# Attention scores on one core: the second rotary product of two key tiles in the two halves of TensorE's array

## The chip, the core and the metric

The kernel runs on one core of a Trainium2 chip. The core has five engines with a queue each: TensorE (PE) multiplies matrices on an array of 128 by 128 cells and writes its sums into PSUM, VectorE (DVE), ScalarE (ACT) and GpSimd (POOL) work element by element, and SyncE (SP) mostly issues DMA. A matmul consists of two instructions: a weight load (shown as PEld), which puts up to 128 x 128 values into the array, and the product itself, which streams up to 512 columns past them. The metric is the device time of one execution in microseconds; the median of three runs of the kernel before is 1282.82 us.

## What is computed

One layer of an encoder over 2048 tokens: an input projection, four heads of gated linear attention, four heads of latent attention with a rotary part, an output projection, a residual sum and a layer norm. The change concerns the scores of the latent attention:

```python
s = (jnp.einsum('bqhd,bkhd->bhqk', qn, k_nope, preferred_element_type=jnp.float32)
     + jnp.einsum('bqhr,bkr->bhqk', qr, k_r, preferred_element_type=jnp.float32))
p = jax.nn.softmax(s, axis=-1)
return jnp.einsum('bhqk,bkhv->bqhv', p.astype(v.dtype), v)
```

The rotary key `k_r` has 64 entries per token and is shared by the four heads; `qr` is the rotary query of one head.

## The kernel before

Float32 products are made from two parts. `hi` (L397) rounds a value to TensorE's fast 32-bit type on ACT, `lo` (L404) takes the rest as a second value of that type on DVE or POOL, and a product is the sum of high x high, high x low and low x high; low x low is left out (`mm3`, L452 to L456).

The program runs in stages. The sweeps over 128-token chunks project the input, do the linear attention and leave what the latent attention needs: in SBUF, for each of the 16 chunks (key tiles) `c`, the compressed keys `ckvT_h[:, c]` and `ckvT_l[:, c]` (128 x 128 each), their untransposed forms `vh`, `vl`, and one tile `kr[:, c]` (printed as krs) for the rotary key; in DRAM the absorbed queries and the rotary queries, high and low.

The rotary key has 64 entries, half of the array's rows. So `kr` stacks both parts: `c_krsh` (L1416, on ACT) writes the high part of a chunk's rotary key into columns 0 to 63 of a small tile, `c_krsl` (L1420, on POOL) the low part into columns 64 to 127, `c_tm` (L1433) transposes it on PE, and `c_krT` puts it into `kr[:, c]`: rows 0 to 63 hold the high part, rows 64 to 127 the low part. `fetch` (L1629) loads a query block's rotary part twice, into rows 0 to 63 and rows 64 to 127 of `rh` (high) and of `rl` (low). One product of `kr` with `rh` over all 128 rows thus gives (high + low) x high, and one with `rl` gives (high + low) x low.

Attention goes over 16 blocks (512 queries of one head), each over 8 pairs `j` of key tiles. `scores(i, j)` writes the two tiles of a pair into the two banks of one PSUM tile `pS` (two such tiles in rotation), five products of 512 columns each: three over the compressed part, `rh`, `rl`. Then `copy` brings both banks to SBUF in one ACT instruction (L1649), `smax` keeps the running maximum on DVE (L1662); once a block's 8 pairs are there the maximum is transposed and spread (`mx`, `mb`), subtracted on DVE (L1686), exponentiated on ACT (L1690), split on ACT (`phi`) and POOL (`plo`), and multiplied with the values on PE (`pv`, six products per pair into `o`). `acc` sums the exponentials on DVE and POOL. Blocks overlap: while one block's scores are made, the block before is in its softmax.

The order of all this is written by hand: the table `PLACE` gives each step a place in units of pairs, the steps are sorted by it, and `in_order` keeps every engine's instructions in that order. So no scheduler decides anything when a step becomes longer or shorter. The last block has its own table, and POOL also gets pieces of the output projection's preparation (`PLACE_OUT`) between the attention steps from block 9 on.

Of the kernel before, what the change touches and what calls it, by code (L numbers as in the profile page):

```python
# [92 lines left out]
    half=11.7,  # L93
# [296 lines left out]
class K:  # L390
# [1024 lines left out]

    def c_krsh(self, d):  # L1416
        d["krs"] = self.w1.tile([P, 2, 64], F32R, tag="krs", name=f"krs{d['c']}")
        self.hi(d["krs"][:, 0], d["kr"][:, 0])

    def c_krsl(self, d):  # L1420
        self.lo(d["krs"][:, 1], d["kr"][:, 0], d["krs"][:, 0], "pool")

    def c_vh(self, d):
        self.hi(self.vh[:, d["c"]], d["ckv"])
# [181 lines left out]
    def attention(self):  # L1606
        tc, nc = self.tc, self.nc
        mm = nc.tensor.matmul
        V, G, Ac = nc.vector, nc.gpsimd, nc.scalar
        NP = NKT // 2  # L1610
        with ExitStack() as ctx:
# [20 lines left out]
            def scores(i, j):  # L1632


                d = stt[i]
                qh, ql, rh, rl = d["q"]
                ps = d["ps", j] = pS.tile([P, 2, QB], F32, tag="pS", name=f"pS{i}_{j}")
                for e in range(2):
                    kh, kl, kr = (t[:, 2 * j + e] for t in (self.ckvT_h, self.ckvT_l, self.kr))
                    mm(ps[:, e], kh, qh, start=True, stop=False)  # L1640
                    mm(ps[:, e], kh, ql, start=False, stop=False)  # L1641
                    mm(ps[:, e], kl, qh, start=False, stop=False)  # L1642
                    mm(ps[:, e], kr, rh, start=False, stop=False)  # L1643
                    mm(ps[:, e], kr, rl, start=False, stop=True)  # L1644

            def copy(i, j):
                d = stt[i]
# [193 lines left out]
            for i in range(nb):  # L1841
                for j in range(NP):
                    t = NP * i + j
                    put(t, scores, i, j)
                    for n, f in (("copy", copy), ("max", smax), ("sub", sub), ("exp", exp), ("hi", phi), ("lo", plo),
                                 ("pv", pv), ("acc", acc)):
                        if n != "acc" or j != SUM_POOL[0] or i == nb - 1:
                            put(t + at(n, i, j), f, i, j)
                put(NP * i + at("acc0", i), acc0, i)
                for n, f in (("tmax", tmax), ("rmax", rmax), ("bmax", bmax)) + {nb - 1: (), nb - 2: own_late}.get(i, own):  # L1850
                    put(NP * i + NP - 1 + at(n, i), f, i)
                if i + 2 < nb:
                    put(NP * i + 4.05, fetch, i + 2)
# [103 lines left out]
            half = 5.44  # L1957
# [466 lines left out]
```

## Time and profile before

| what | value |
| --- | --- |
| median of 3 runs | 1282.82 us (1281.37 to 1285.22) |
| the profiled execution | 1283.54 us |
| its span, first to last instruction | 1281.7 us |
| mean granted TensorE clock | 0.998 |
| first and last score product | 607.9 and 1084.4 us |
| score products | 5 lines x 256 |
| copies of a pair (L1649) | 128 |

A row of a group reads: line, engine, operation, output<-inputs, shapes, count | busy time, mean ns of one | idle time of the engine just before, and who ended it. A row of the timeline begins with start and duration in us. Ends of matmuls are modelled: a matmul's duration overlaps its successor's, so what one costs is read from the starts. A row by stretches gives, for each engine, the busy time within the stretch and the number of instructions.

### The profile page before, as it was taken

What the parts mean: (1) busy time and instruction counts of PE and PEld (TensorE: products, weight loads), DVE (VectorE), ACT (ScalarE), POOL (GpSimd) and SP (SyncE); (2) the same over time, 40 slices, a digit from 0 to 9 for tenths busy, and PEclk for the clock granted to TensorE, in tenths of its full rate; (3) what the DMA queues carried; (4) which work ended last, traced back from release to release, by engine and by line L of the source; (5) the groups of instructions that cost most, each with busy time, mean ns of one, the idle gap of its engine ahead of it and who ended that gap; (6) DMA issues with size and microseconds to landing.
All of it is one profiled execution on the core that took longest, in us unless ns stands there. A gap on an engine that the chain in (4) does not pass through costs nothing.

```text
span 1281.7 us, 20184 instructions
## 1 busy us (share of the span) xinstructions
PE 1255.0 (98%) x6928; PEld 1108.3 (86%) x6928; DVE 941.1 (73%) x1702; ACT 876.2 (68%) x1553; POOL 852.7 (67%) x550
## 2 busy tenths in 40 slices
PE   7999999999999999999999999999999999999996
PEld 7999999999889999999788888888888888788875
DVE  7865775656675445555798888888888889648887
ACT  7765657666675665665588888888888888623355
POOL 0245555363657666672188888889999999955784
PEclk9999999999999999999999999999999999999999
DMA  8332525253675565555501111122213221468962
GB/s 299 98 92 63 177 71 172 87 155 101 195 244 159 180 225 189 181 194 166 175 1 41 42 42 41 42 58 58 59 58 91 53 52 33 173 211 304 343 196 84
DMA packets 122518, 166.81 MB, mean 130 GB/s; under 512 B 18502, under 2 KB 71118, under 8 KB 121776
## 3 DMA queue, kind: packets, MB, share of 16 engines
q1 hardware_dynamic: 114256, 163.39, 40.2%
q0 software_dynamic: 768, 2.10, 0.5%
q8 instruction: 55, 0.90, 0.4%
q10 hardware_dynamic: 7392, 0.03, 0.3%
q14 instruction: 47, 0.39, 0.2%
HBM read 106.72 MB, written 58.75 MB: 129 GB/s over the span
## 4 chain that ended last, share of the span: by engine, by line
PE 75%; DVE 6%; ACT 5%; POOL 4%; DMA 3%; issue 3%; SPq 0%; DVEq 0%; POOLq 0%; ACTq 0%
PE pS L1640 4%; PE pS L1641 4%; PE pS L1642 4%; PE pS L1643 4%; PE pS L1644 4%; PE o L454 4%; PE o L455 4%; PE o L456 4%; PE ipa L454 3%; PE ipa L456 3%; PE ipa L455 3%; PE pz L455 2%; PE pz L456 2%; PE pz L454 2%; PE ipg L454 2%
## 5 line engine op out<-in xcount | busy, mean ns | idle before, releaser
L406 POOL TENSOR_TENSOR pl<-s,ph 128x1024 fp32r<-128x1024 f32 x128 | 306.3, 2417 | 56.3 <-ACT ph L400 56.3
L1662 DVE TENSOR_TENSOR rm<-pS,rm 128x512 f32<-128x512 f32 x210 | 144.8, 690 | 26.4 <-ACT s L1649 20.8
L1686 DVE TENSOR_TENSOR s<-s,mb 128x1024 f32<-128x1024 f32 x128 | 151.3, 1214 | 9.4 <-PE mb L1680 9.3
L1649 ACT ACTIVATE s<-pS 128x1024 f32<-128x1024 f32 x128 | 131.3, 1026 | 37.7 <-PE pS L1644 33.4
L400 ACT ACTIVATE ph<-s 128x1024 fp32r<-128x1024 f32 x128 | 134.9, 1057 | 13.5 <-PE o L456 12.7
L1690 ACT ACTIVATE s<-s 128x1024 f32<-128x1024 f32 x128 | 131.5, 1050 | 13.4 <-DVE s L1686 13.3
L454 PE MATMUL ipa<-wah,xah 128*128 128x384 f32 (+1 forms) x384 | 129.8, 338 | 6.3 <-ACT wah L400 6.3
L1103 POOL TENSOR_TENSOR Us<-Us,cw 128x512 f32<-128x512 f32 x16 | 18.6, 1164 | 173.4 <-DVE Us L1101 157.9
L456 PE MATMUL ipa<-wah,xal 128*128 128x384 f32 (+1 forms) x384 | 124.8, 325 | 0.0
L455 PE MATMUL ipa<-wal,xah 128*128 128x384 f32 (+1 forms) x384 | 124.5, 324 | 0.1
L1640 PE MATMUL pS<-qh,ckvT_h 128*128 128x512 f32 x256 | 102.6, 401 | 0.8 <-DVE rm L1662 0.4
L454 PE MATMUL o<-ph,vh 128*128 128x512 f32 x256 | 101.1, 395 | 0.0
L1641 PE MATMUL pS<-ql,ckvT_h 128*128 128x512 f32 x256 | 99.9, 390 | 0.0
L1642 PE MATMUL pS<-qh,ckvT_l 128*128 128x512 f32 x256 | 99.9, 390 | 0.0
L1643 PE MATMUL pS<-rh,krs 128*128 128x512 f32 x256 | 99.8, 390 | 0.0
L1644 PE MATMUL pS<-rl,krs 128*128 128x512 f32 x256 | 99.8, 390 | 0.0
L456 PE MATMUL o<-ph,vl 128*128 128x512 f32 x256 | 99.8, 390 | 0.0
L455 PE MATMUL o<-pl,vh 128*128 128x512 f32 x256 | 99.7, 390 | 0.0
L1713 DVE TENSOR_TENSOR ap<-ap,s 128x512 f32<-128x512 f32 x120 | 83.1, 693 | 3.5 <-ACT s L1690 0.9
L454 PEld LDWEIGHTS ipa<-wah,xah 128*128 128x128 f32 x384 | 73.0, 190 | 7.1 <-ACT wah L400 6.5
L454 PE MATMUL pz<-xch,wzh 128*128 128x256 f32 x256 | 74.8, 292 | 0.0
L455 PEld LDWEIGHTS ipa<-wal,xah 128*128 128x128 f32 x384 | 73.0, 190 | 1.2 <-DVE wal L406 0.6
(446 smaller groups left out, 3902.2 us busy)
## 6 DMA issues: line engine op xcount, KB each, us to landing
xcf<-xT_dram SPq DMA_DIRECT2D x16, 512.0 KB, 4.7
xr<-x_dram SPq DMA_DIRECT2D x16, 512.0 KB, 6.3
xaf<-xT_dram SPq DMA_DIRECT2D x14, 512.0 KB, 3.8
wb<-wO_dram SPq DMA_DIRECT2D x16, 256.0 KB, 3.0
oib<-oi_s SPq DMA_DIRECT2D x16, 256.0 KB, 3.7
qdb<-qd_s SPq DMA_DIRECT2D x16, 256.0 KB, 4.8
SU<-su_s SPq DMA_DIRECT2D x16, 256.0 KB, 4.6
ub<-u_s SPq DMA_DIRECT2D x16, 256.0 KB, 4.2
```

The costliest lines, as they stand in the source:

```text
L400: return nc.scalar.activation(dst, src, AF.Copy).ins
L406: return e.tensor_tensor(dst, src, hi.bitcast(F32), ALU.subtract).ins
L454: mm(out, ah, bh, start=start, stop=False)
L455: mm(out, ah, bl, start=False, stop=False)
L456: mm(out, al, bh, start=False, stop=stop)
L1640: mm(ps[:, e], kh, qh, start=True, stop=False)
L1641: mm(ps[:, e], kh, ql, start=False, stop=False)
L1642: mm(ps[:, e], kl, qh, start=False, stop=False)
L1643: mm(ps[:, e], kr, rh, start=False, stop=False)
L1644: mm(ps[:, e], kr, rl, start=False, stop=True)
L1662: V.tensor_tensor(d["rm"], src[:, e], d["rm"], ALU.max)
L1686: V.tensor_tensor(s, s, d["mb"][:, None, :].to_broadcast([P, 2, QB]), ALU.subtract)
```

## The change

The product over `rl` is taken out of the loop over the two tiles of a pair and put behind it, and each of the two now uses 64 rows: the even tile rows 0 to 63, the odd tile rows 64 to 127 of `kr` and `rl`. So that these rows hold the high part in both cases, odd chunks get their high part in columns 64 to 127 and their low part in columns 0 to 63. The term low x low, which the products over 128 rows added, is no longer computed.

```diff
     def c_krsh(self, d):
         d["krs"] = self.w1.tile([P, 2, 64], F32R, tag="krs", name=f"krs{d['c']}")
-        self.hi(d["krs"][:, 0], d["kr"][:, 0])
+        self.hi(d["krs"][:, d["c"] % 2], d["kr"][:, 0])
 
     def c_krsl(self, d):
-        self.lo(d["krs"][:, 1], d["kr"][:, 0], d["krs"][:, 0], "pool")
+        p = d["c"] % 2
+        self.lo(d["krs"][:, 1 - p], d["kr"][:, 0], d["krs"][:, p], "pool")
...
                     mm(ps[:, e], kh, ql, start=False, stop=False)
                     mm(ps[:, e], kl, qh, start=False, stop=False)
                     mm(ps[:, e], kr, rh, start=False, stop=False)
-                    mm(ps[:, e], kr, rl, start=False, stop=True)
+                for e in range(2):
+                    half = slice(64 * e, 64 * e + 64)
+                    mm(ps[:, e], self.kr[half, 2 * j + e], rl[half], start=False, stop=True)
```

How PE's order changes is seen in the sixth block, where its sixth pair of scores is followed by the product of the block before with the values. Line numbers behind the edit are larger by one (sweep) or by three (from the second half of `scores` on). Before (pS is the pair's PSUM tile, o the output of the block before, the sizes are those of the result):

```order
L456 MATMUL o_9352<-ph_0_9278,vl 128x512
L1640 MATMUL pS_5_9368<-qh_8784,ckvT_h 128x512
L1641 MATMUL pS_5_9368<-ql_8786,ckvT_h 128x512
L1642 MATMUL pS_5_9368<-qh_8784,ckvT_l 128x512
L1643 MATMUL pS_5_9368<-rh_8788,krs 128x512
L1644 MATMUL pS_5_9368<-rl_8791,krs 128x512
```

The five rows of pS stand there twice, once per tile, and then `o` goes on. With the change, from the second tile's last compressed product on:

```order
L1643 MATMUL pS_5_9368<-qh_8784,ckvT_l 128x512
L1644 MATMUL pS_5_9368<-rh_8788,krs 128x512
L1647 MATMUL pS_5_9368<-rl_8791,krs 128x512 x2
L454 MATMUL o_9352<-ph_1_9313,vh 128x512
L455 MATMUL o_9352<-pl_1_9349,vh 128x512
L456 MATMUL o_9352<-ph_1_9313,vl 128x512
```

The first tile's product over rl has moved past four products of the second tile and stands next to the second tile's.

The other neighbour that the halves have is the transpose of a block's maximum, `mx`, in the first pair of the 15th block (`mx` and `o` belong to blocks before it). Before:

```order
L1643 MATMUL pS_0_11717<-rh_11304,krs 128x512
L1644 MATMUL pS_0_11717<-rl_11307,krs 128x512
L1668 MATMUL mx_11734<-ident,rm_11481 128x128 x4
L454 MATMUL o_11598<-ph_4_11642,vh 128x512
L455 MATMUL o_11598<-pl_4_11715,vh 128x512
```

With the change:

```order
L1644 MATMUL pS_0_11717<-rh_11304,krs 128x512
L1647 MATMUL pS_0_11717<-rl_11307,krs 128x512 x2
L1671 MATMUL mx_11734<-ident,rm_11481 128x128 x4
L454 MATMUL o_11598<-ph_4_11642,vh 128x512
L455 MATMUL o_11598<-pl_4_11715,vh 128x512
```

Nothing else moved here; the two products over rl stand between a product over all rows and a transpose. The instructions of ACT, DVE, POOL and SP stand in the same order with the same waits as before.

## The prediction

> **What bounds the kernel now.** I read the page first: busy times, then the chain of work that ended last.
>
> ```profile
> PE 1255.0 (98%) x6928; PEld 1108.3 (86%) x6928; DVE 941.1 (73%) x1702; ACT 876.2 (68%) x1553; POOL 852.7 (67%) x550
> PE 75%; DVE 6%; ACT 5%; POOL 4%; DMA 3%; issue 3%; SPq 0%; DVEq 0%; POOLq 0%; ACTq 0%
> L1640 PE MATMUL pS<-qh,ckvT_h 128*128 128x512 f32 x256 | 102.6, 401 | 0.8 <-DVE rm L1662 0.4
> L1643 PE MATMUL pS<-rh,krs 128*128 128x512 f32 x256 | 99.8, 390 | 0.0
> L1644 PE MATMUL pS<-rl,krs 128*128 128x512 f32 x256 | 99.8, 390 | 0.0
> L1649 ACT ACTIVATE s<-pS 128x1024 f32<-128x1024 f32 x128 | 131.3, 1026 | 37.7 <-PE pS L1644 33.4
> ```
>
> TensorE (PE) holds three quarters of the chain. The score products run 256 times per line: 16 blocks of 16 key tiles, 128 pairs (the copy at L1649, one per pair, says x128). In all of them PE sat idle 0.8 us before L1640 and 0.0 before the others, while ScalarE (ACT) waited 33.4 us for L1644. So within the attention stage the others wait for PE and PE for nobody. The busy times by stretch, from the first score to the last and then to the end, say the same and show who is next:
>
> ```profile
> core 0: us, PE busy (x) PEld busy (x) DVE busy (x) ACT busy (x) POOL busy (x), PEclk, DMA share, GB/s
> 607.90:700.00 92.10, 90.20 (x407) 73.27 (x406) 76.83 (x102) 69.55 (x78) 56.08 (x24) 1.00 0.26 78
> 700.00:800.00 100.00, 100.00 (x457) 82.58 (x457) 89.92 (x126) 84.61 (x95) 84.86 (x36) 1.00 0.16 40
> 800.00:900.00 100.00, 100.00 (x457) 82.67 (x456) 88.94 (x123) 84.41 (x95) 88.20 (x38) 1.00 0.19 51
> 900.00:1000.00 100.00, 100.00 (x460) 82.63 (x460) 88.01 (x122) 85.58 (x98) 92.88 (x41) 1.00 0.28 79
> 1000.00:1084.50 84.50, 84.50 (x385) 69.81 (x384) 76.89 (x107) 73.80 (x85) 83.25 (x40) 1.00 0.14 33
> 1084.50:1281.70 197.20, 186.41 (x837) 153.11 (x835) 145.23 (x226) 93.05 (x213) 135.01 (x89) 0.98 0.65 215
> ```
>
> PE is full in four of the five score stretches, at full granted clock (1.00). A nanosecond more per pair on PE is therefore a nanosecond of kernel; a nanosecond less counts only until GpSimd (POOL), busy 83.25 of 84.50 us in the last stretch, becomes the bound.
>
> What a matmul costs is not the 390 ns of the groups, since matmuls overlap. The timeline of one pair gives the step between starts (PEld are the weight loads):
>
> ```profile
> 709.15 0.39 PE L1640 MATMUL pS<-qh,ckvT_h 128*128 128x512 f32 x1
> ...
> 709.83 0.39 PE L1643 MATMUL pS<-rh,krs 128*128 128x512 f32 x1
> 709.84 0.19 PEld L1644 LDWEIGHTS pS<-rl,krs 128*128 128x128 f32 x1
> 710.06 0.39 PE L1644 MATMUL pS<-rl,krs 128*128 128x512 f32 x1
> ...
> 711.19 0.39 PE L1644 MATMUL pS<-rl,krs 128*128 128x512 f32 x1
> ...
> 711.87 0.39 PE L1642 MATMUL pS<-qh,ckvT_l 128*128 128x512 f32 x1
> ```
>
> From 709.15 to 711.87 lie twelve steps: 2.72 / 12 = 0.227 us each. A matmul prints 0.39 us, so 0.390 - 0.227 = 0.163 us of it runs under its successor. A weight load prints 0.19 us (187/188 ns at L1644) and runs under the matmul before it.
>
> **The change part by part.** *Removed and added.* Each pair loses two whole-array products over rl (2 x 0.227 us) and gains two products of half the rows, one in rows 0 to 63, one in rows 64 to 127. If the halves run side by side, both take one step of 0.227 us, since each still streams 512 columns. The gain is 0.227 us per pair, 128 x 0.227 = 29.0 us. If they run one after the other the gain is nothing.
>
> *The layout changes.* PE now goes from the whole array to halves and back, once per pair: 256 changes. No instruction of before uses half the rows, so I bound the price of one change by the nearest rows. The nearest odd shape is a four-column weight load, in the stretch behind the scores; a row of plain transposes stands beside it:
>
> ```profile
> 1106.75 0.39 PE L456 MATMUL o<-ph,vl 128*128 128x512 f32 x1
> 1106.98 0.27 PE L1785 MATMUL rt<-ident,rc 128*4 128x128 f32 x1
> 1107.01 0.48 PE L454 MATMUL o<-ph,vh 128*128 128x512 f32 x1
> 1107.32 0.40 PE L455 MATMUL o<-pl,vh 128*128 128x512 f32 x1
> ...
> 305.57 0.38 PE L984 MATMUL qT<-ident,q 128*128 128x128 f32 x2
> 305.79 0.38 PE L1019 MATMUL kT<-ident,k 128*128 128x128 f32 x2
> ```
>
> From 1106.75 to 1107.32 are 0.57 us; two steps of 0.227 leave 0.116 us for the odd shape, and a plain transpose takes (305.79 - 305.57) / 2 = 0.11 us. So that shape cost nothing extra: the low end is 0. (Below nothing it cannot go: a change computes nothing, and the shared step is counted above.) The high end: the array must first be empty, 0.163 us of tail exposed, and only then are the next weights loaded, 0.188 us: 0.351 us. I take 0.163 us: the odd shape keeps all 128 rows and writes one output at a time, so it asks for no such change as the halves do, and the tail is the one row that tells how long a product is still under way behind its step. That the loads are then hidden I take from the row at 709.84, where one runs fully under another matmul.
>
> *The second half's weights.* Two transposes 0.11 us apart show how closely weight loads can follow each other. The second half starts between 0 and 0.11 us behind the first; I take 0, as both loads (0.22 us) fit under the step of the matmul ahead. At the other end it is 14.1 us over 128 pairs.
>
> The Trainium skill bears on this in two places that speak against the change. Its page TensorEngine Tiling (Array Packing), section Key Properties, states that a change of tiling mode, unlike a change of tile, drains TensorE; no run here shows it yet. Its page TensorE: Matmul & The Clock Gate, section Single matmul latency, gives a lone warm matmul as (398 + N) / 2.4 ns, so 166 ns beyond the streaming, against the trace's 163 ns; by the page the sum below would be 128 x (2 x 0.166 - 0.227) = +13.4 us, an estimate.
>
> *What moves.* The first tile's bank closes four products later, 4 x 0.227 = 0.9 us. This costs nothing: its reader is the one copy over both banks (128x1024, L1649), which needs the second bank as well, and the maxima on VectorE (DVE) come behind the copy. Were the banks copied apart, the first copy would slide 0.9 us and with it the maximum. The other engines' orders and waits are the same as before. In the first pair, the two DMAs that bring rl are now waited for by one half each, later than before; nothing is late.
>
> *High and low swapped in odd tiles.* The same two instructions per chunk write the other 64 columns: same engines, shapes and count, cost 0; the transposes that follow read all 128 columns either way, and the product over rh sums both parts in either order.
>
> *Sum.* 128 x (2 x 0.163 - 0.227) = 41.7 - 29.0 = +12.7 us. The profiled execution took 1283.5 us for a span of 1281.7, 0.7 us above the median. 1283.5 + 12.7 - 0.7 = 1295.5 us. PE has no slack in these stretches to take it up (1.9 us idle in the first), and behind the last score the work follows PE in order.
>
> **The rivals.**
>
> *Faster: the change of layout is free and the halves run side by side.* Then PE loses 29.0 us over a stage of 476.6 us, 6.1%. The stretches would shrink from 92.1 to 86.5 and from 100 to 93.9 us in three, the third of these to 94.5 with POOL at 92.88; the last stretch stops at POOL's 83.25 (PE alone: 79.4). Together 5.6 + 6.1 + 6.1 + 5.5 + 1.2 = 24.5 us, so 1258.3 us; without POOL's limit 1253.8. For it speaks the odd shape that passed at 0.116 us; against it that no half of the rows was in use there. The rival holds while a change costs under 0.113 us (half of 0.227); at 0.05 us each, 1266.6 us. The Trainium skill, TensorE: Matmul & The Clock Gate, Part 3, has row tiles starting about 4 ns apart and four products of 32 rows done 3.07 times as fast; the halves would by that cost 0.231 us, an estimate of -28.5 us before POOL; it does not price the way back to the whole array.
>
> *Much slower: the weights are loaded behind the emptied array.* A change then costs 0.163 + 0.11 = 0.273 us (the closest loads seen) to 0.351 us: 256 x 0.273 - 29.0 = +40.9 and 256 x 0.351 - 29.0 = +60.9 us, 1323.7 to 1343.7 us. Halves that run one after the other between two drains of 0.163 us land there too, 256 x 0.163 = +41.7 us. For it: the loads now hide only because a matmul runs beside them. Against it: weights of another layout need not wait for sums of the old one to leave.
>
> *No change: the halves are treated as whole products.* One after the other, each 0.227 us, without price for a change: 1282.8 us. A change price near 0.113 us gives the same time. For it speaks that fewer rows have bought nothing so far: a product that reads 98 of them takes about as long as a transpose over 128.
>
> ```profile
> L925 PE MATMUL z<-lrTs,wg 98*128 98x128 f32 x64 | 9.1, 264 | 0.8 <-ACT lrTs L400 0.8
> L1668 PE MATMUL mx<-ident,rm 128*128 128x128 f32 x60 | 9.0, 272 | 0.3 <-DVE rm L1662 0.3
> ```
>
> Against it: 98 rows leave no room for a second product, 64 do; and for a price that just cancels the gain the window is narrow.
>
> **How the numbers follow.** Forecast (drain hidden loads, price 0.13 to 0.20 us, own range 1287 to 1305 us): 0.37. Much slower: 0.19. Faster: 0.36. No change: 0.08. A measurement of this kernel tells about 0.3% (3.9 us) from no change, 30 ns per pair. Faster by over 0.3%: 0.36; within: 0.08; slower: 0.37 + 0.19 = 0.56. The range takes in the faster rival's free end with POOL's limit, 1256, and the near end of the much slower one, 1325; what is left out is the rest of that one (some 0.12) and little below (0.03).
>
> **What would show it.** In the changed trace the two products over rl start within 0.01 us of each other if the halves run side by side, 0.11 us if the loads space them, 0.227 us if not at all. The starts from L1643's last product (L1644 there) to the first whole one behind the halves should be 2 x 0.227 + 2 x 0.163 = 0.78 us for the forecast, 0.45 us for the faster rival, 1.0 us or more for the much slower. PE should still be full in the score stretches and DVE, ACT and POOL show more idle time; if instead POOL fills the last stretch and PE waits at L455 for pl, the faster rival holds. The weight loads behind the halves show whether they start under them. The forecast is wrong if a change costs under 0.113 us or if the loads are exposed too.

## The result and the profile after

The changed kernel took 1304.4 us (median of 4 runs, 1303.9 to 1304.86) against 1283.0 us before: the ratio is 1.0165, with a 95% interval of 1.0148 to 1.0183. It is 21.4 us slower; 12.7 us were forecast. The profiled execution has a span of 1303.0 us, 21.3 us more than before.

Where the time went is seen in three stretches: up to the first score product, the score stage, and the rest. First the kernel before, then the changed one (columns as in the windows of the prediction):

```profile
0.00:607.60 607.60, 593.62 (x3933) 563.96 (x3934) 375.13 (x900) 385.07 (x894) 312.41 (x286) 1.00 0.50 160
607.60:1084.70 477.10, 475.20 (x2164) 391.43 (x2163) 420.95 (x577) 398.13 (x448) 405.47 (x177) 1.00 0.21 57
1084.70:1281.70 197.00, 186.21 (x836) 152.95 (x834) 145.03 (x226) 92.97 (x212) 134.81 (x88) 0.98 0.65 215
```

```profile
0.00:607.90 607.90, 594.48 (x3932) 564.68 (x3933) 373.94 (x900) 384.99 (x894) 312.26 (x286) 1.00 0.50 160
607.90:1106.00 498.10, 496.60 (x2161) 357.25 (x2159) 420.10 (x577) 399.82 (x448) 406.57 (x177) 1.00 0.20 54
1106.00:1303.00 197.00, 186.70 (x838) 153.39 (x837) 145.28 (x226) 93.08 (x213) 133.28 (x88) 0.99 0.65 215
```

The stages in front of and behind the scores are as long as they were. The score stage grew from 477.1 to 498.1 us, 21.0 us or 0.164 us per pair. DVE, ACT and POOL are busy in it for the same time as before to within 2 us, and PE stays full: PE sets the pace and takes longer. The other engines wait more, as the groups of the changed kernel's page show:

```profile
L1652 ACT ACTIVATE s<-pS 128x1024 f32<-128x1024 f32 x128 | 131.4, 1026 | 53.6 <-PE pS L1647 51.0
L454 PE MATMUL o<-ph,vh 128*128 128x512 f32 x256 | 107.7, 421 | 0.0
L1641 PE MATMUL pS<-qh,ckvT_h 128*128 128x512 f32 x256 | 105.3, 411 | 0.6 <-ACT s L1693 0.4
L1644 PE MATMUL pS<-rh,krs 128*128 128x512 f32 x256 | 99.8, 390 | 0.0
```

ACT's copy now waits 51.0 us for the halves, where it waited 33.4 us for L1644. A tile's view of the instructions over rl and one place of the timeline show what happens on PE:

```profile
L1647 PEld LDWEIGHTS pS<-rl,krs x256: 182/183/183, 610.3 to 1106.0; 64*128 64x128 f32 x128
L1647 PE MATMUL pS<-rl,krs x256: 492/498/502, 610.3 to 1106.0; 64*128 64x512 f32 x128
```

```profile
709.89 0.39 PE L1643 MATMUL pS<-qh,ckvT_l 128*128 128x512 f32 x1
710.12 0.39 PE L1644 MATMUL pS<-rh,krs 128*128 128x512 f32 x1
710.43 0.19 PEld L1647 LDWEIGHTS pS<-rl,krs 64*128 64x128 f32 x2 [0.35 <-issue]
710.43 0.50 PE L1647 MATMUL pS<-rl,krs 64*128 64x512 f32 x2
710.86 0.19 PEld L454 LDWEIGHTS o<-ph,vh 128*128 128x128 f32 x1 [0.25 <-issue]
710.87 0.50 PE L454 MATMUL o<-ph,vh 128*128 128x512 f32 x1
710.97 0.19 PEld L455 LDWEIGHTS o<-pl,vh 128*128 128x128 f32 x1
711.20 0.39 PE L455 MATMUL o<-pl,vh 128*128 128x512 f32 x1
```

The two halves stand in one row, x2, 0.50 us from the first start to the last end, while a single one prints 498 ns: they run at the same time. Over all 128 pairs of the trace the second half starts 3 or 4 ns behind the first. Before them, and again behind them, the weight loader sits idle, 0.35 and 0.25 us, and "issue" means that it waits for no other engine. The halves' loads start 0.31 us after the last whole product did (0.318 us in the median of all 128 pairs), so 0.09 us after that product's step of 0.227 us is over. A load that starts together with its product is hidden by nothing: a product that prints 0.39 us prints 0.50 us here, 0.11 us more. This is the open load and nothing peculiar to halves, as one place of the kernel before shows, where PE had waited for ACT and a whole product starts together with its load; its successor comes 0.33 us behind it:

```profile
624.10 0.19 PEld L1640 LDWEIGHTS pS<-qh,ckvT_h 128*128 128x128 f32 x1 [0.44 <-ACT s L1649]
624.10 0.50 PE L1640 MATMUL pS<-qh,ckvT_h 128*128 128x512 f32 x1
624.43 0.39 PE L1641 MATMUL pS<-ql,ckvT_h 128*128 128x512 f32 x1
```

The same happens in the changed kernel on the way back: load and product of L454 start together, 0.43 us behind the halves, and the next product follows after 0.33 us in place of 0.227. From 710.12 to 711.20 are 1.08 us; three steps (last whole, halves, first whole) would take 0.68. The two changes of layout cost 0.40 us, 0.20 us each: 0.09 us until the next load starts and 0.11 us of that load.

The medians of the runs say the same: 21.4 us more in spite of the 29.0 us gained by the shared step make 50.4 us over 256 changes, 0.197 us each.

### The profile page after: what moved, and what is told of

Same layout as the page of the kernel before. It is cut to its first block, busy times and chain, and to the rows that moved or that the text cites. A ratio compares the mean times of both kernels' runs of the same rounds, so it can differ in the third digit from the quotient of the medians.

```text
span 1303.0 us, 20168 instructions
## 1 busy us (share of the span) xinstructions
PE 1277.8 (98%) x6928; PEld 1075.3 (83%) x6928; DVE 939.3 (72%) x1702; ACT 877.9 (67%) x1553; POOL 852.1 (65%) x550
## 4 chain that ended last, share of the span: by engine, by line
PE 56%; POOL 4%; issue 3%; DVE 3%; ACT 2%; DMA 1%; SPq 0%; DVEq 0%; POOLq 0%; ACTq 0%
PE o L454 5%; PE pS L1641 5%; PE o L455 4%; PE o L456 4%; PE pS L1642 4%; PE pS L1644 4%; PE pS L1643 4%; PE pS L1647 4%; PE pz L455 2%; PE pz L456 2%; PE pz L454 2%; PE ipm L456 1%; PE ipm L454 1%; PE ipm L455 1%; PE mx L1671 1%
## 5 line engine op out<-in xcount | busy, mean ns | idle before, releaser
L454 PE MATMUL ipa<-wah,xah 128*128 128x384 f32 (+1 forms) x384 | 130.4, 340 | 6.2 <-ACT wah L400 6.1
L454 PE MATMUL o<-ph,vh 128*128 128x512 f32 x256 | 107.7, 421 | 0.0
L1641 PE MATMUL pS<-qh,ckvT_h 128*128 128x512 f32 x256 | 105.3, 411 | 0.6 <-ACT s L1693 0.4
L1644 PE MATMUL pS<-rh,krs 128*128 128x512 f32 x256 | 99.8, 390 | 0.0
L454 PEld LDWEIGHTS ipa<-wah,xah 128*128 128x128 f32 x384 | 73.3, 191 | 7.2 <-ACT wah L400 6.7
L454 PE MATMUL pz<-xch,wzh 128*128 128x256 f32 x256 | 74.8, 292 | 0.0
L455 PE MATMUL pz<-xcl,wzh 128*128 128x256 f32 x256 | 72.8, 285 | 0.3 <-POOL xcl L406 0.3
```

Source lines behind the costliest of these rows:

```text
L454: mm(out, ah, bh, start=start, stop=False)
L455: mm(out, ah, bl, start=False, stop=False)
```

## The experiments

Each kernel's time stands beside runs of the kernel before on the same chip; those medians lay between 1282.0 and 1283.7 us. The edits of reorder, twice, one_half, joined, delayed and delayed_ps are shown against the changed kernel, the others against the kernel before; `...` stands for lines left out.

**reorder**: the change's order and swap, whole products.

```diff
                 for e in range(2):
-                    half = slice(64 * e, 64 * e + 64)
-                    mm(ps[:, e], self.kr[half, 2 * j + e], rl[half], start=False, stop=True)
+                    mm(ps[:, e], self.kr[:, 2 * j + e], rl, start=False, stop=True)
```

> The change with its order and its swap of high and low, but the two products over rl read all 128 rows again, so PE never leaves the whole-array layout. Theory (the price lies in the two layout changes per pair, about 0.20 us each: 0.09 us until the array is free and 0.11 us of a weight load that nothing hides): back at the time of before, 1283 us, within 2 us. Rival (the order costs: the first bank closes later, or the two rl products next to each other are late): stays above 1290 us.

Measured: 1283.1 us, ratio 1.0005 (0.9995 to 1.0015). Moving the first tile's product past four others and swapping high and low in odd tiles cost nothing that can be measured. All of the loss comes from the 64 rows.

**same_rows**: without the swap, both tiles in rows 0 to 63.

```diff
-                    mm(ps[:, e], kr, rl, start=False, stop=True)
+                for e in range(2):
+                    mm(ps[:, e], self.kr[0:64, 2 * j + e], rl[0:64], start=False, stop=True)
```

> Without the swap: both tiles' products over rl use rows 0 to 63 of the array, one behind the other, so there are two layout changes per pair as in the change, but nothing can run side by side. Theory (halves of different rows run side by side in one step of 0.227 us): 128 x 0.227 = 29 us above the change, about 1333 us. Rival (in the change the halves already run one after the other, whatever the trace's starts say): no different from the change, 1304 us.

Measured: 1333.2 us, 28.8 us above the change. In the same rows the two products follow one another; in different rows the second is free, as "one_half" below shows once more.

**twice**: the pair of halves issued twice.

```diff
-                for e in range(2):
-                    half = slice(64 * e, 64 * e + 64)
-                    mm(ps[:, e], self.kr[half, 2 * j + e], rl[half], start=False, stop=True)
+                for n in range(2):
+                    for e in range(2):
+                        half = slice(64 * e, 64 * e + 64)
+                        mm(ps[:, e], self.kr[half, 2 * j + e], rl[half], start=False, stop=n == 1)
```

> The change with the pair of half products issued twice (even, odd, even, odd tile), so the term over rl is added twice and the output is not the reference's; still two layout changes per pair. Theory (the price belongs to the change, and a further pair of halves costs one step): 128 x 0.227 = 29 us above the change, about 1333 us. Rival (the price belongs to every half product, 0.31 us each): 128 x 0.63 = 80 us above, about 1384 us. Rival (halves one after the other): 58 us above, 1362 us.

Measured: 1336.2 us (1333.8 to 1338.6), 31.8 us above the change, 0.25 us per pair. The two runs lie 4.8 us apart, so this does not differ from the 29 us expected: the second pair of halves in an open period costs about one step. The price belongs to the change of layout, not to the product. The timeline of this run, for comparison with the one above (0.32 us in, 0.66 for four halves in place of 0.43 for two, 0.34 out):

```profile
714.44 0.39 PE L1644 MATMUL pS<-rh,krs 128*128 128x512 f32 x1
714.76 0.73 PE L1648 MATMUL pS<-rl,krs 64*128 64x512 f32 x4
715.42 0.50 PE L454 MATMUL o<-ph,vh 128*128 128x512 f32 x1
715.76 0.39 PE L455 MATMUL o<-pl,vh 128*128 128x512 f32 x1
```

**apart**: each half behind its own tile, rows 0 to 63, four changes per pair.

```diff
-                    mm(ps[:, e], kr, rl, start=False, stop=True)
+                    mm(ps[:, e], self.kr[0:64, 2 * j + e], rl[0:64], start=False, stop=True)
```

> Half products as in the even tile for both tiles, each at its old place behind its own tile's four whole products: four layout changes per pair in place of two, nothing side by side. Theory (0.20 us per change): per pair 2 x 0.227 + 4 x 0.20 in place of 2 x 0.227, so 128 x 0.80 = 102 us above before, about 1385 us. Rival (the price belongs to the products, two per pair here as in the change): 128 x 0.40 = 51 us above before, about 1334 us.

Measured: 1383.3 us, ratio 1.0787 (1.0765 to 1.0808), 100.6 us above before. Nothing is shared here, so the 100.6 us are 512 changes, 0.196 us each: the same price as from the change itself, by another way.

**one_half**: the change without the odd tile's product over rl.

```diff
-                    mm(ps[:, e], kr, rh, start=False, stop=False)
-                for e in range(2):
-                    half = slice(64 * e, 64 * e + 64)
-                    mm(ps[:, e], self.kr[half, 2 * j + e], rl[half], start=False, stop=True)
+                    mm(ps[:, e], kr, rh, start=False, stop=e == 1)
+                half = slice(0, 64)
+                mm(ps[:, 0], self.kr[half, 2 * j], rl[half], start=False, stop=True)
```

> The change without the odd tile's product over rl (left out, so the odd tiles' scores lack that term). Theory (the second half runs under the first): as the change, 1304 us, within 2 us. Rival (the second half's weight load, 0.11 us, lengthens the period): 128 x 0.11 = 14 us less, 1290 us. Rival (halves one after the other): 29 us less, 1275 us.

Measured: 1304.0 us, against 1304.4 us for the change. The second half costs nothing that can be measured, its weight load included.

**rows96**: the kernel before with products over 96 rows.

```diff
-                    mm(ps[:, e], kr, rl, start=False, stop=True)
+                    mm(ps[:, e], self.kr[0:96, 2 * j + e], rl[0:96], start=False, stop=True)
```

> The kernel before with its products over rl cut to 96 rows (the high part and half of the low part; part of low x low is left out), each at its old place. Theory (what costs is the change between the whole array and its halves, which 96 rows do not ask for): as before, 1283 us, within 2 us. Rival (any product of fewer than 128 rows pays): like the four changes per pair of the run with the halves apart, far above 1300 us.

Measured: 1288.4 us, ratio 1.0042 (1.0026 to 1.0059). Fewer than 128 rows alone do not bring the price; but it is not "as before, within 2 us" either. The 4.8 us are 19 ns per product. The timeline shows the loads hidden as ever and steps of 0.23 to 0.24 us around the short product:

```profile
711.40 0.40 PE L1644 MATMUL pS<-rl,krs 96*128 96x512 f32 x1
711.63 0.40 PE L1640 MATMUL pS<-qh,ckvT_h 128*128 128x512 f32 x1
711.87 0.40 PE L1641 MATMUL pS<-ql,ckvT_h 128*128 128x512 f32 x1
712.10 0.39 PE L1642 MATMUL pS<-qh,ckvT_l 128*128 128x512 f32 x1
```

Over all places of the trace where whole products follow, the four steps from the short product on have medians of 232, 238, 232 and 231 ns in place of 227: the loss lies in them, and not in the step into the short product (227). Behind the halves of "apart" nothing of the kind is seen beyond the two long steps (227 ns again). What causes it stays open.

**one_whole**: the kernel before without the odd tile's product over rl: what a free change of layout would have brought.

```diff
-                    mm(ps[:, e], kr, rh, start=False, stop=False)
-                    mm(ps[:, e], kr, rl, start=False, stop=True)
+                    mm(ps[:, e], kr, rh, start=False, stop=e == 1)
+                    if e == 0:
+                        mm(ps[:, e], kr, rl, start=False, stop=True)
```

> The kernel before without the odd tile's product over rl (left out, so the odd tiles' scores lack that term): what the change would have brought if a change of layout cost nothing. Theory (PE gains 29.0 us until POOL is full in the last stretch): 24.5 us below before, 1258 us. Rival (POOL does not bind, PE's gain counts in full): 1254 us. Rival (the fixed order makes PE wait for others long before): above 1265 us.

Measured: 1268.7 us, ratio 0.9889 (0.9870 to 0.9909), 14.9 us below before. About half of the 29.0 us is lost. At the end of the score stage POOL, the last of the five busy times, is full for 68.69 of 69.00 us, as the prediction had it for its last stretch:

```profile
900.00:1000.00 100.00, 99.77 (x449) 80.00 (x448) 93.33 (x130) 88.60 (x103) 96.64 (x43) 1.00 0.28 80
1000.00:1069.00 69.00, 67.73 (x299) 53.02 (x299) 62.24 (x89) 59.44 (x70) 68.69 (x34) 1.00 0.14 35
```

But the loss begins long before. Counted from the first score product of a block to that of the next, blocks 5 to 13 take 29.6 to 29.7 us in place of 30.9, 1.2 to 1.3 us less where 8 x 0.227 = 1.8 us were to be gained, and POOL is busy for 26.1 to 28.5 us of each. PE prints as full there (99.77 us), since a product's printed tail covers a short stop. The waits of PE's weight loader in the score stage say whom it waits for; the first fence is the kernel before, the second this run (who waited for whom: us in total, times, longest):

```profile
PEld pS L1640 <- ACT s L1690: 1.6, 2, 0.8
PEld mb L1680 <- DVE mc L1673: 1.0, 1, 1.0
PEld mx L1668 <- DVE rm L1662: 0.7, 1, 0.7
PEld pS L1640 <- ACT s L1649: 0.4, 1, 0.4
```

```profile
PEld o L454 <- DVE ofl L406: 7.2, 14, 0.9
PEld pS L1640 <- ACT s L1691: 3.9, 5, 1.3
PEld pS L1640 <- ACT ph L400: 3.1, 11, 0.3
PEld pS L1640 <- issue: 2.8, 15, 0.3
PEld mb L1681 <- DVE mc L1674: 1.5, 3, 1.0
PEld mx L1669 <- DVE rm L1663: 1.5, 1, 1.5
PEld o L455 <- POOL pl L406: 1.1, 4, 0.3
```

They grew from 3.7 to 21.1 us. The largest comes 14 times, about once per block: the single bank of `o` is read by DVE (ofl) before the next block may write it. Its 0.5 us each is as much as the middle blocks lack; that it is the cause is read from the waits, and a second bank for `o` was not tried. Only 1.1 us are waits named for POOL's pl.

**joined**: one layout period per two pairs, the odd pair's halves opening its sums early.

```diff
+                ps, odd = d["ps", j], j % 2 == 1
...
-                    mm(ps[:, e], kh, qh, start=True, stop=False)
+                    mm(ps[:, e], kh, qh, start=not odd, stop=False)
...
-                    mm(ps[:, e], kr, rh, start=False, stop=False)
-                for e in range(2):
-                    half = slice(64 * e, 64 * e + 64)
-                    mm(ps[:, e], self.kr[half, 2 * j + e], rl[half], start=False, stop=True)
+                    mm(ps[:, e], kr, rh, start=False, stop=odd)
...
+            def joined(i, j):
+                d = stt[i]
+                rl = d["q"][3]
+                d["ps", j + 1] = pS.tile([P, 2, QB], F32, tag="pS", name=f"pS{i}_{j + 1}")
+                for n in range(2):
+                    for e in range(2):
+                        half = slice(64 * e, 64 * e + 64)
+                        mm(d["ps", j + n][:, e], self.kr[half, 2 * (j + n) + e], rl[half], start=n == 1, stop=n == 0)
...
+                    if j % 2 == 0:
+                        put(t + 0.3, joined, i, j)
```

> The halves of two neighbouring pairs are issued together: behind the whole products of the even pair come its two halves and then the two halves of the odd pair, which open that pair's sums; the odd pair's whole products follow later. One layout period per two pairs in place of two. Theory (0.20 us per change, one step per side-by-side pair): per two pairs 2 x 0.227 + 2 x 0.20 = 0.85 us in place of 0.91 us of before, so 64 x 0.054 = 3.4 us below before, about 1280 us, if PE does not have to wait for the odd pair's PSUM tile, which is now needed some 1.4 us earlier. Rival (a fixed price per half product): no better than the change, 1304 us. Rival (the earlier need of the tile makes PE wait for the maximum that still reads it): in between, with idle time before the second pair of halves.

Measured: 1312.4 us, ratio 1.0228 (1.0213 to 1.0243), worse than the change. The wait of the third expectation is there, though the time is not in between but above the change: PE waits between the two pairs of halves for the maximum that still reads the buffer which the odd pair's tile needs, 25.1 us in all, and where it waits the two pairs do not follow each other at one step.

```profile
L1655 PE MATMUL pS<-rl,krs 64*128 64x512 f32 x256 | 54.8, 464 | 25.1 <-DVE rm L1673 25.1
```

One such wait in the timeline, between the even pair's halves and the odd pair's:

```profile
706.19 0.50 PE L1655 MATMUL pS<-rl,krs 64*128 64x512 f32 x2
706.38 1.41 DVE L1673 TENSOR_TENSOR rm<-pS,rm 128x512 f32<-128x512 f32 x2
...
707.93 0.50 PE L1655 MATMUL pS<-rl,krs 64*128 64x512 f32 x2 [1.24 <-DVE rm L1673]
```

**delayed** and **delayed_whole**: joined the other way round, the odd pair's whole products early, and the maximum reading the copies; the second of the two with whole products. Both have the first two parts of this edit; only delayed has the third, with a `joined` that issues the halves of both pairs to end their sums.

```diff
-                src = s if i == 0 else ps
+                src = s
...
-                    put(t, scores, i, j)
+                    put(t if j % 2 == 0 else t - 0.72, scores, i, j)
...
+                    if j % 2 == 0:
+                        put(t + 0.30, joined, i, j)
```

> Joined the other way round: the odd pair's whole products come early, right behind the even pair's, and then the halves of both pairs in one layout period; the maximum reads the copies in SBUF, so that a PSUM tile is free once it is copied. One layout period per two pairs, no tile needed before its turn by the maximum. Theory: 64 x (2 x 0.227 + 2 x 0.20 - 4 x 0.227) = 64 x -0.054 = 3.4 us below before, 1280 us, if the order costs nothing; by what the same order costs with whole products (the run beside it) this shifts. Rival (a price per half product): at or above 1304 us.

> The same order of the pairs and the same reading of the maximum with the whole products of before, no halves: what the order alone costs. Theory: the run with the joined halves lies 3.4 us below this one, wherever the order puts it. If the order is free: 1283 us. Rival (the order with two pairs of scores in a row makes PE wait for the copies): above 1290 us.

Measured: 1562.8 and 1536.2 us. Neither says anything of halves. In delayed_whole DVE is busy for 608.5 of the 693.0 us from 607 to 1300 us, since a maximum with both inputs in SBUF took 1677 ns on average in place of 690; PE waits for the maxima, and its granted clock reads 0.88 and 0.86 in the two parts of this stretch, against 1.00 before.

**delayed_ps** and **delayed_whole_ps**: the same with the maximum reading PSUM.

> The delayed joining again, with the maximum reading PSUM as in the kernel before (from SBUF on both sides it took 1.68 us in place of 0.69 us and DVE became the bound). Theory (0.20 us per change of layout, two changes per two pairs): 3.4 us below the run beside it with the same order and whole products; 1280 us if that order is free. Rival (a price per half product): 21 us above the run beside it. If PE waits for the copies and maxima in both, the difference is blurred, and the idle time before L1640 in the two traces says so.

> The order of the run beside it with whole products and the maximum from PSUM: what the order alone costs. Theory: 1283 us if the PSUM tiles come free in time; up to 1300 us if PE waits for the odd pair's tile, which it now needs 2.5 us earlier.

Measured: 1402.1 and 1334.6 us, and neither expectation holds. The order alone costs some 51 us, as PE waits for maxima and ACT; with halves it costs 67 us more, neither 3.4 us less nor 21 us more. The score stage is 594.1 us long with halves and 528.0 without; PE's waits in it are 87 and 44 us, and the granted clock reads 0.96 and 1.00. Why the waits are longer is argued and not tried: probably the first of the joined pairs now also ends later. These two kernels are not full on PE, so the difference is no price of a change. That one period for two pairs pays on this kernel was not shown. From "twice" and "apart", two pairs would by estimate take 0.23 + 0.25 + 2 x 0.20 = 0.88 us against 0.91 us before, 2 us for the whole kernel if nothing waited; that is less than the 4.8 us between the two runs of "twice", and every order tried made PE wait for more than that. None of the versions beats the kernel before with its whole computation.

## Why the prediction was right, and where its terms were off

*PE bounds the score stage, a nanosecond more is a nanosecond of kernel*: held; 21.0 of 21.3 us fell there with PE full.

*The halves run side by side in one step*: held, by the starts 3 or 4 ns apart, by "same_rows" (28.8 us for the loss of it, 29.0 worked out) and by "one_half" (no difference). *The second half starts at once*: held, within the 0.01 us that the prediction asked for.

*The move and the swap cost nothing*: held ("reorder", 1.0005).

*The price of a layout change, 0.163 us*: direction right, size too small; it measured 0.197 us, and 256 x 0.034 = 8.7 us are the whole gap between the 12.7 us forecast and the 21.4 us found. Both of its parts were wrong, in opposite directions. The forecast exposed the whole printed tail, 0.163 us; the loads began 0.09 us after the step. And it took the loads as hidden, from a row in which a load runs under a product of the same layout; across a change of layout they lie open, 0.11 us each. That second part was the much slower rival's, with its near price of 0.11 us for a load; its tail was too long, so it landed at 1323.7 us. The truth took one part from each.

So the mechanism is only half right. The prediction named the exposed loads as a sign that the forecast is wrong, and they are exposed. That 1304.4 us still lies in the forecast's own range, 0.6 us below its end, is partly luck: a tail 0.07 us too long stood in for most of a load left out. The other sign misleads: the starts from L1644's last product to the first whole one behind the halves are 0.75 us apart, close to the forecast's 0.78, but the first whole product's open load shows only in the step behind it, 0.33 us.

The pages cited with the forecast: that a change of tiling mode drains TensorE (the Trainium skill, TensorEngine Tiling (Array Packing), Key Properties) agrees with the trace in kind, the loader idle for 0.35 us before the halves and 0.25 us behind them. The 166 ns that the prediction cites from the Trainium skill, TensorE: Matmul & The Clock Gate, Single matmul latency (given there for a bf16 product), was not the length of the drain: 0.09 us could be seen, and the load behind it is not in that figure.

*The faster rival*: it failed on the price, 0.197 us against the 0.113 us at which it ends. Its own sum was off too. "one_whole" brought 14.9 us, not 24.5. POOL does bind at the end of the score stage; what failed is the step that PE's gain counts in full until POOL becomes the bound: the middle blocks lose 0.5 of their 1.8 us each, with POOL not full. Busy shares alone do not say how much of a faster PE survives.

*No change*: the halves are not treated as whole products.

## What to carry to other kernels

Price the way into and out of a special layout of the array, not only the work done in it: here 0.20 us each way, nearly a whole 512-column product, so that a period has to save at least two product steps before it pays. When weight loads are hidden, ask under which instruction they hide, and whether that cover is still there for the first product on the other side. A gain on the bounding engine should be tried by leaving the work out before a way to save it is built: this showed that, in this order, some 15 of 29 us were to be had (interval 12 to 17).

## What was not expected of the hardware

A whole-layout product over 96 rows made the kernel 4.8 us slower (0.4%), 19 ns per product, although its duration reads 0.40 us against 0.39 to 0.40 of its neighbours. And a maximum on DVE over two SBUF inputs took 681 to 2928 ns, with a median of 1958, in a stretch where POOL works as well, against a median of 691 ns with one input in PSUM. The view of the tile rm gives minimum, median and maximum in ns; first the run delayed_whole, then the kernel before:

```profile
L1662 DVE TENSOR_TENSOR rm<-s,rm x224: 681/1958/2928, 614.1 to 1334.1; 128x512 f32<-128x512 f32 x112
```

```profile
L1662 DVE TENSOR_TENSOR rm<-s,rm x14: 691/692/969, 615.0 to 628.5; 128x512 f32<-128x512 f32 x14
L1662 DVE TENSOR_TENSOR rm<-pS,rm x210: 680/691/695, 634.8 to 1086.7; 128x512 f32<-128x512 f32 x105
```

In the kernel before, the first block reads the maximum from SBUF on both sides too, at 692 ns; no pl of an earlier block is made beside it yet. Its one slow maximum of 969 ns is the one that begins while POOL has work:

```profile
623.21 1.29 POOL L406 TENSOR_TENSOR wv_l<-wvf,wv_h 128x512 fp32r<-128x512 f32 x1 [15.80 <-ACT wv_h L400]
624.08 0.97 DVE L1662 TENSOR_TENSOR rm<-s,rm 128x512 f32<-128x512 f32 x1 [2.01 <-ACT s L1649]
```

The trace of delayed_whole parts its 240 maxima over two SBUF inputs in the same way: the 73 that meet no work of POOL take at most 695 ns, and the 120 that take over 1 us all overlap it by more than 1 us. DVE's additions with one input in PSUM (L1713), 73 of which run wholly beside POOL's work, stay between 673 and 700 ns. No run leaves POOL's work out, but in these traces the slow maxima come with it and not without it.
